# Depthwise convolution: six of its 47 half-length taps as ScalarE products, summed by adding DMAs; contiguous even and odd accumulators

## The chip, the cores and the metric

The program runs on one core of a Trainium2 chip. Five engines work side by side, each through its own queue in order: TensorE (PE, matrix products), VectorE (DVE), ScalarE (ACT), GpSimd (POOL) and SyncE (SP). SP and POOL issue the DMA transfers. An instruction that waits for a semaphore holds back everything behind it in its own queue. The metric is the device time of one execution in microseconds (us).

## What is computed

One step of a hybrid decoder layer, for a prompt of 1024 positions and 8 sample requests of 8 positions each. The part that the change touches is branch B, a causal depthwise convolution with 31 taps over 1024 channels, between a gated product and a LayerNorm:

```python
xn = rmsnorm(x, norm1_g)
q, k, v, glu_a, glu_b, gate_a, gate_b = split(xn @ w_in)
branch_a = swa_attention(q, k, v, sinks) @ w_o_attn
u = glu_a * sigmoid(glu_b)
c = dwconv_valid(concat([conv_b_past, u]), conv_b_w, conv_b_bias)   # 31 taps per channel
branch_b = silu(layernorm(c, ln_b_g, ln_b_b)) @ w_pb
h = x + (sigmoid(gate_a) * branch_a + sigmoid(gate_b) * branch_b) @ w_out
y = h + conv_ffn(rmsnorm(h))
```

All arithmetic is float32. Each product of matrices is made of three (high by high, high by low, low by high), and this is why TensorE has so much to do.

## The kernel before

**Stages.** The first 640 us are the input projection with everything that hangs on it: weights are taken one 128-column block after another, each multiplied with all 1088 positions (in chunks of 384, 384 and 320) into PSUM banks, of which there are four under the tag `mm` and four under `aux`. What leaves the banks is rounded and split into two words by ACT and DVE (`q`, `k`, `v`) or turned into the gated input `u`. The LayerNorm and the other projections follow, and the second half of the run is the convolutional FFN.

**The convolution.** Channels are taken in 8 tiles of 128, on the partitions. When `u` of tile i is complete, `a_done` calls `conv(i, u)` with a low priority (`CONV_LATER`), so that the scheduler strews its instructions among those of the projections and, from some 200 us on, of attention. The eight convolutions follow each other from 66 to 619 us. Even and odd positions are computed apart by three sums of half length, 512 positions: `bt` (even inputs by even taps, 513 wide), `ye` (odd inputs by odd taps), `yo` (sums of neighbouring inputs, `sm`, by sums of neighbouring taps, `hsum`). That is 16 + 15 + 16 = 47 taps of half length instead of 62. The first tap of each sum is written by ACT (L555 to L557); the other 44 are multiply-adds on DVE (`mac`, L545), each reading and writing its accumulator. `ye` and `yo` are the even and odd columns of one tile `c`, so their elements are two apart; `bt` is a tile of its own. Then the sums are combined into `out`, inside `u` (L565 to L567), and POOL stores it to DRAM as `d_c` (L568, L569). The LayerNorm (`ln_steps`, L571 on) loads `d_c` once the last of the eight stores has landed.

**What stands around it in the queues.** On DVE: the low words of weights (`wlo`, L183) and of `q` and `k` (L787, L809), the softmax (L392, an instruction of its own kind), the low words of the transposed probabilities (`ptl`, L237). On ACT: the high words (L182, L786, L236), the exponentials (L397), their scaling (L401). On POOL: a copy of a column for each softmax (`p<-nsink`, L386), the stores of the gates (L767), of attention (L468, L469), loads of cached keys and values (L479, L480) and the stores of the convolution. Tiles of a tag are reused in turn: `u` has two buffers, `p` two, `c`, `sm` and `bt` one each.

Adding DMAs exist in the kernel at three other places, all later: L1202 (`ml` from DRAM into SBUF), L1463 through L1456 (`d_b`, from SBUF to DRAM) and L1919 (`H`).

Of the kernel before, what the change touches and what calls it, by code (L numbers as in the profile page):

```python
# [8 lines left out]
AF = mybir.ActivationFunctionType  # L9
ALU = mybir.AluOpType  # L10
AX = mybir.AxisListType

P = 128
DM = 1024
KT = DM // P
SEQ = 1024
# [64 lines left out]
SQUARES_LATER = 3000  # L81
W_PARTS = 4
CONV_LATER = 1200
TURN_SOONER = -60
LN_AT = ((0, 1, 17, 36), (2, 37, 50, 80), (60, 81, 103, 134), (90, 135, 152, 183))
LEAD = (0, 0)
# [42 lines left out]
class Build:  # L129
# [273 lines left out]
    def attn_unit(self, p, blk, st):  # L403
# [22 lines left out]
        def turn(g, kb):  # L426
# [5 lines left out]
            pl = self.t(self.at, [P, 512], "ptl", F32R, bufs=2)  # L432
            with self.later(TURN_SOONER if self.now - self.gated <= 3 else 0):
                self.split_ps(ph, pl, ps)
# [98 lines left out]
    def conv(self, i, u):  # L533
        nc = self.nc
        half = SEQ // 2
        acc = self.t(self.cv, [P, T], "c")
        sm = self.t(self.cv, [P, half + 15], "sm")
        bt = self.t(self.cv, [P, half + 1], "bt")
        us = u[:, PW:].rearrange("p (b t) -> p b t", b=NB)
        sp = acc[:, SEQ:].rearrange("p (b t) -> p b t", b=NB)  # L540
        ev, od = u[:, 0:PW:2], u[:, 1:PW:2]
        ye, yo = acc[:, 0:SEQ:2], acc[:, 1:SEQ:2]
        h = lambda k: self.c("cw", i * CW + k)
        hs = lambda j: self.hsum[:, 16 * i + j:16 * i + j + 1]
        mac = lambda o, x, w: nc.vector.scalar_tensor_tensor(o, x, w, o, ALU.mult, ALU.add)  # L545
        taps = self.c("cw", i * CW, CW)[:, None, None, :].to_broadcast([P, NB // 2, NT, CW])
        prod = acc[:, 0:NS // 2 * CW].rearrange("p (b t k) -> p b t k", b=NB // 2, k=CW)
        for x in range(2):
            win = us[:, 4 * x:4 * x + 4, 0:NT]
            win = bass.AP(tensor=win.tensor, offset=win.offset, ap=[list(z) for z in win.ap] + [[1, CW]])  # L550
            nc.vector.tensor_tensor(prod, win, taps, ALU.mult)
            nc.vector.tensor_reduce(sp[:, 4 * x:4 * x + 4, :], prod, AX.X, ALU.add)
        nc.vector.tensor_tensor(sm, od[:, 0:half + 15], ev[:, 1:half + 16], ALU.add)
        act = nc.scalar.activation
        act(bt, ev[:, 0:half + 1], AF.Identity, scale=h(0))  # L555
        act(ye, od[:, 0:half], AF.Identity, bias=self.c("cb", i), scale=h(1))
        act(yo, sm[:, 0:half], AF.Identity, bias=self.cb2[:, i:i + 1], scale=hs(0))  # L557
        for j in range(1, 16):
            mac(bt, ev[:, j:j + half + 1], h(2 * j))
            if j < 15:  # L560
                mac(ye, od[:, j:j + half], h(2 * j + 1))
            mac(yo, sm[:, j:j + half], hs(j))
        out = u[:, NS:NS + SEQ]
        nc.vector.tensor_scalar(u[:, 0:NS], acc[:, SEQ:], self.c("cb", i), None, ALU.add)
        nc.vector.tensor_tensor(yo, yo, bt[:, 1:], ALU.subtract)  # L565
        nc.vector.tensor_tensor(out[:, 1::2], yo, ye, ALU.subtract)
        nc.vector.tensor_tensor(out[:, 0::2], ye, bt[:, 0:half], ALU.add)  # L567
        nc.gpsimd.dma_start(self.d_c[i, :, 0:SEQ], out)  # L568
        nc.gpsimd.dma_start(self.d_c[i, :, SEQ:], u[:, 0:NS])  # L569
# [123 lines left out]
    def phase_x(self):  # L693
# [46 lines left out]
        def a_done(i, u):  # L740
            us = u_views(u)
            nc.gpsimd.dma_start(a["o_cbp"][i], u[:, SEQ:SEQ + HIST])
            nc.gpsimd.dma_start(a["o_cbs"][i], us[:, :, NT:])
            with self.later(CONV_LATER):
                self.conv(i, u)
# [1443 lines left out]
```

## Time and profile before

| | us |
|---|---|
| median of 3 runs | 1640.43 (1640.31 to 1640.95) |
| span of the profiled execution | 1640.2 |
| PE busy | 1631.0 |
| DVE busy | 1401.0 |
| ACT busy | 880.5 |
| POOL busy | 262.9 |
| the 352 MACs of the convolutions (L545), busy | 262.8 |

The profiled execution's own time was that of its span, 1640.2 us from the first instruction to the last, and the granted TensorE clock was 0.999 over it. A row of a group names the line, the engine, the operation, the tile written and those read, shapes and count; then its busy time and the mean of one in ns; then the idle time in front and what ended most of it. A row of the timeline has the start in us and the duration, and in square brackets the idle time before it, if there was any. `L545` is line 545 of the kernel before. In the new kernel the lines up to `conv` stand 2 further down, the conv's `mac` is L547, its starts L557 to L559, and from its combining sums on all lines stand 12 further down (L809 is L821).

### The profile page before, as it was taken

To read this page: it belongs to the slowest core of one execution; us is meant where nothing else is said; L and a number is where in the kernel's file an instruction comes from. 1 tells how busy PE (TensorE), PEld (TensorE's weight loads), DVE (VectorE), ACT (ScalarE), POOL (GpSimd) and SP (SyncE) were. 2 spreads that over 40 slices of the span, in tenths; PEclk is the share of its full clock that TensorE was granted. 3 is DMA by queue.
4 is the path that set the end of the run, shared out by engine and by line. 5 is a ranking of instruction groups with operands and counts; after the bars stand their busy time and mean duration, and the time that the engine had idled before them with its cause. 6 is when DMAs were issued, how large, how long until landed. Compare 5 with 4: busy or idle time off the path is not lost.

```text
span 1640.2 us, 30212 instructions
## 1 busy us (share of the span) xinstructions
PE 1631.0 (99%) x11540; PEld 1615.4 (98%) x11540; DVE 1401.0 (85%) x2597; ACT 880.5 (54%) x1845; POOL 262.9 (16%) x549
## 2 busy tenths in 40 slices
PE   9999999999999999999999999999999999999998
PEld 9999999999999999999999999999999999999998
DVE  7899979999979996778755999988888887989867
ACT  6524277774488754666532465555555555524322
POOL 0100111222011101111102422222222111000000
PEclk9999999999999999999999999999999999999999
DMA  6221222323121256548763631344444334766423
GB/s 211 85 59 54 64 74 58 106 83 114 43 70 42 90 181 196 174 152 233 185 226 108 214 119 63 112 117 115 115 117 118 99 112 142 255 165 163 110 62 110
DMA packets 104857, 201.58 MB, mean 123 GB/s; under 512 B 25992, under 2 KB 56712, under 8 KB 104696
## 3 DMA queue, kind: packets, MB, share of 16 engines
q1 hardware_dynamic: 81528, 131.47, 26.4%
q0 software_dynamic: 22752, 67.79, 13.8%
q8 instruction: 90, 1.47, 0.4%
q14 instruction: 55, 0.45, 0.1%
q10 hardware_dynamic: 432, 0.40, 0.1%
HBM read 137.55 MB, written 64.03 MB: 123 GB/s over the span
## 4 chain that ended last, share of the span: by engine, by line
PE 89%; DVE 5%; ACT 3%; DMA 1%; issue 1%; SPq 0%; POOLq 0%; DVEq 0%; ACTq 0%
PE mm L201 21%; PE mm L202 21%; PE mm L203 21%; PE aux L203 7%; PE aux L202 7%; PE aux L201 7%; PE aux L430 1%; DVE c L545 1%; PE aux L443 1%; PE aux L444 1%; DMA ct<-d_c 1%; PE aux L420 1%; PE aux L421 1%; DVE bt L545 1%; ACT ct L625 1%
## 5 line engine op out<-in xcount | busy, mean ns | idle before, releaser
L201 PE MATMUL mm<-xh,whi 128*128 128x384 f32 (+1 forms) x904 | 301.4, 333 | 0.3 <-ACT xh L290 0.3
L202 PE MATMUL mm<-xl,whi 128*128 128x384 f32 (+1 forms) x904 | 295.3, 327 | 0.2 <-DVE xl L291 0.2
L203 PE MATMUL mm<-xh,wlo 128*128 128x384 f32 (+1 forms) x904 | 295.4, 327 | 0.0
L202 PEld LDWEIGHTS mm<-xl,whi 128*128 128x128 f32 x904 | 170.0, 188 | 1.2 <-DVE xl L291 0.5
L201 PEld LDWEIGHTS mm<-xh,whi 128*128 128x128 f32 x904 | 169.9, 188 | 1.3 <-ACT xh L290 0.6
L203 PEld LDWEIGHTS mm<-xh,wlo 128*128 128x128 f32 x904 | 169.7, 188 | 0.1
L1435 DVE SCALAR_TENSOR_TENSOR acc<-st,fc,acc 128x1104 f32<-128x1104 f32 x88 | 119.9, 1365 | 12.2 <-issue 6.7
L182 ACT CAST whi<-wraw 128x1024 fp32r<-128x1024 f32 (+1 forms) x62 | 59.6, 967 | 65.2 <-PE mm L202 51.3
L203 PE MATMUL mm<-th,wlo 128*128 128x272 f32 x320 | 92.4, 289 | 0.0
L201 PE MATMUL mm<-th,wlo 128*128 128x272 f32 x320 | 92.4, 289 | 0.0
L202 PE MATMUL mm<-tl,wlo 128*128 128x272 f32 x320 | 92.4, 289 | 0.0
L545 DVE SCALAR_TENSOR_TENSOR bt<-u,consts,bt 128x513 f32<-128x513 f32 x120 | 89.7, 748 | 0.7
L545 DVE SCALAR_TENSOR_TENSOR c<-sm,hsum,c 128x512 f32<-128x512 f32 x120 | 89.5, 746 | 0.7
L203 PE MATMUL mm<-mh,wlo 128*128 128x272 f32 (+4 forms) x304 | 89.2, 293 | 0.0
L545 DVE SCALAR_TENSOR_TENSOR c<-u,consts,c 128x512 f32<-128x512 f32 x112 | 83.6, 746 | 0.5
L236 ACT CAST whi<-wraw 128x512 fp32r<-128x512 f32 x76 | 47.5, 625 | 61.5 <-DVE wraw L1631 26.4
L183 DVE TENSOR_TENSOR wlo<-wraw,whi 128x1024 fp32r<-128x1024 f32 (+1 forms) x62 | 68.9, 1116 | 7.2 <-ACT whi L182 6.9
L1780 ACT COPY st<-mm 128x272 f32<-128x272 f32 (+2 forms) x132 | 43.8, 349 | 56.9 <-PE mm L203 56.9
L236 ACT CAST wlo<-wraw 128x512 fp32r<-128x512 f32 x76 | 47.4, 624 | 40.7 <-PE mm L203 17.9
L397 ACT ACTIVATE p<-p,nm 128x257 f32<-128x257 f32 (+1 forms) x128 | 62.3, 490 | 11.9 <-DVE nm L392 11.4
L1433 ACT ACTIVATE acc<-st,fc 128x1104 f32<-128x1104 f32 x44 | 57.6, 1314 | 15.3 <-DVE st L1736 11.9
L201 PE MATMUL aux<-mh,whi 128*128 128x272 f32 (+4 forms) x216 | 63.9, 296 | 0.0
(712 smaller groups left out, 5764.9 us busy)
## 6 DMA issues: line engine op xcount, KB each, us to landing
wraw<-wall SPq DMA_DIRECT2D x118, 512.0 KB, 3.8
bw<-d_b SPq DMA_DIRECT2D x42, 272.0 KB, 3.8
d_b<-gd POOLq DMA_DIRECT2D x36, 272.0 KB, 6.1
d_b<-acc POOLq DMA_DIRECT2D x24, 272.0 KB, 4.9
ar<-wdn SPq DMA_DIRECT2D x32, 192.0 KB, 3.8
d_g<-acc POOLq DMA_DIRECT2D x10, 544.0 KB, 4.4
ga<-d_ga SPq DMA_DIRECT2D x8, 544.0 KB, 5.2
ct<-d_c SPq DMA_DIRECT2D x8, 544.0 KB, 6.3
```

The costliest lines, as they stand in the source:

```text
L182: self.cast = self.nc.scalar.copy(h[:, z], r[:, z]).ins
L183: self.nc.vector.tensor_tensor(l[:, z], r[:, z], h[:, z].bitcast(F32), ALU.subtract)
L201: mm(ps, wh, xh, start=first, stop=False, skip_group_check=more)
L202: mm(ps, wh, xl, start=False, stop=False, skip_group_check=more)
L203: self.last_mm = mm(ps, wl, xh, start=False, stop=last, skip_group_check=more).ins
L236: self.cast = self.nc.scalar.copy(h, src).ins
L397: nc.scalar.activation(pt[:, j, lo:width + 1], pt[:, j, lo:width + 1], AF.Exp, bias=nm[:, j:j + 1], scale=-1.0, accum_out=den[:, j:j + 1])
L420: nc.tensor.matmul(ps[:, j, :], q[g][:, h, qs], kd[g][:, keys], start=True, stop=False)
L545: mac = lambda o, x, w: nc.vector.scalar_tensor_tensor(o, x, w, o, ALU.mult, ALU.add)
L1433: nc.scalar.activation(acc, st[:, 0:AW], AF.Identity, bias=fb(f), scale=fw(f, 0))
L1435: nc.vector.scalar_tensor_tensor(acc, st[:, k:k + AW], fw(f, k), acc, ALU.mult, ALU.add)
L1780: self.evicted = (add if second and n == 0 and j == 1 else op)(d, r(banks[bank, j]))
```

## The change

Two constants and some fifteen lines in `conv`:

```diff
+ADDED = 6
+TAPS_FIRST = 8
...
-        ye, yo = acc[:, 0:SEQ:2], acc[:, 1:SEQ:2]
+        ye, yo = acc[:, 0:half], acc[:, half:SEQ]
...
         act(yo, sm[:, 0:half], AF.Identity, bias=self.cb2[:, i:i + 1], scale=hs(0))
+        added = ADDED if i else 0
+        for j in range(1, added + 1):
+            tap = self.t(self.at, [P, half], "tap", bufs=2)
+            act(tap, sm[:, j:j + half], AF.Identity, scale=hs(j))
+            nc.gpsimd.dma_start(yo, tap, accum_op=ALU.add)
+        left = list(range(added + 1, 16))
         for j in range(1, 16):
             mac(bt, ev[:, j:j + half + 1], h(2 * j))
             if j < 15:
                 mac(ye, od[:, j:j + half], h(2 * j + 1))
-            mac(yo, sm[:, j:j + half], hs(j))
+            if j > (TAPS_FIRST if added else 0):
+                x = left.pop(0)
+                mac(yo, sm[:, x:x + half], hs(x))
+        for x in left:
+            mac(yo, sm[:, x:x + half], hs(x))
```

In convolutions 1 to 7 (not in 0), taps 1 to 6 of the odd sum `yo` are no longer MACs. ACT multiplies `sm` by the tap into a buffer `tap`, and a DMA from POOL's queue adds the buffer to `yo`, in SBUF. There are two buffers. The other nine MACs of `yo` come later among those of `bt` and `ye`: none before the ninth pair. `ye` and `yo` are the two halves of `c`, each contiguous; `out` is still written in alternating columns. ADDED and TAPS_FIRST are the number of taps so treated and the number of pairs ahead of the first odd MAC.

**VectorE, convolution 1, where its first odd MAC now stands.** `c<-u` is a MAC of the even sum, `c<-sm` one of the odd sum, `bt` the third; `kl` and `q` are low words from the projection. Before:

```order
L545 SCALAR_TENSOR_TENSOR bt_1265<-u_1085,consts_77,bt_1265 128x513
L787 TENSOR_TENSOR q_28_123<-mm_1483,q_28_123 64x256
L545 SCALAR_TENSOR_TENSOR c_1263<-u_1085,consts_77,c_1263 128x512
L545 SCALAR_TENSOR_TENSOR c_1263<-sm_1264,hsum_86,c_1263 128x512
L809 TENSOR_TENSOR kl_143_1517<-mm_1525,kd_141_1515 64x384
```

Now:

```order
L185 TENSOR_TENSOR wlo_153_1534<-wraw_1431,whi_152_1533 128x1024
L799 TENSOR_TENSOR q_27_122<-mm_1495,q_27_122 64x256
L547 SCALAR_TENSOR_TENSOR bt_1265<-u_1085,consts_77,bt_1265 128x513
L799 TENSOR_TENSOR q_28_123<-mm_1495,q_28_123 64x256
L547 SCALAR_TENSOR_TENSOR c_1263<-sm_1264,hsum_86,c_1263 128x512
L547 SCALAR_TENSOR_TENSOR c_1263<-u_1085,consts_77,c_1263 128x512
L821 TENSOR_TENSOR kl_149_1529<-mm_1537,kd_147_1527 64x384
```

Before, an odd MAC stands here that is one of many; now this `c<-sm` is the first of the convolution and waits for the sixth adding DMA, ahead of the same low word of `k`.

**ScalarE, convolution 1, behind the odd sum's start** (`c<-sm` with the bias `cb`). Before:

```order
L557 ACTIVATE c_1263<-sm_1264,cb_17_85,hsum_86 128x512
L786 CAST q_28_123<-mm_1359 64x384
L182 CAST whi_135_1421<-wraw_1324 128x1024
L786 CAST q_27_122<-mm_1388 64x256
L786 CAST q_28_123<-mm_1388 64x256
```

Now:

```order
L559 ACTIVATE c_1263<-sm_1264,cb_17_85,hsum_86 128x512
L798 CAST q_28_123<-mm_1371 64x384
L184 CAST whi_141_1433<-wraw_1336 128x1024
L798 CAST q_27_122<-mm_1400 64x256
L563 ACTIVATE tap_1280<-sm_1264,hsum_86 128x512
L798 CAST q_28_123<-mm_1400 64x256
L804 COPY qs_124<-mm_1400 64x4x2x8 x2
L563 ACTIVATE tap_1283<-sm_1264,hsum_86 128x512
```

The products `tap` stand among the casts that empty the PSUM banks; the two rows shown are the third and fourth product, whose buffers the first and second adding DMA must have read.

**GpSimd, convolution 3**, where it runs beside attention; the semaphores in brackets are those that a row waits for (DMASW: a DMA of this queue). Before:

```order
L767 DMA d_ga_60<-gt_2837 128x384 [waits DMASW5_49,Activation_49]
L767 DMA d_ga_60<-gt_2928 128x320 [waits Activation_49]
L386 COPY p_3122<-nsink_84 128x4 [waits PE_49,Pool_49]
L386 COPY p_3174<-nsink_84 128x4 [waits PE_49,Activation_49,Pool_49]
L479 DMA kp_3551<-kpT 128x256 [waits DMASW0_49,PE_49]
```

Now:

```order
L779 DMA d_ga_60<-gt_2873 128x384 [waits Activation_49]
L564 DMA c_2697<-tap_2708 128x512 [waits DMASW2_49,DVE_49,Activation_49]
L564 DMA c_2697<-tap_2711 128x512 [waits DMASW2_49]
L564 DMA c_2697<-tap_2714 128x512 [waits DMASW4_49,DMASW3_49,Activation_49]
L779 DMA d_ga_60<-gt_2964 128x320 [waits DMASW5_49,Activation_49]
L388 COPY p_3158<-nsink_84 128x4 [waits PE_49,Pool_49]
L564 DMA c_2697<-tap_2717 128x512 [waits DMASW6_49,DMASW4_49,Activation_49]
L388 COPY p_3210<-nsink_84 128x4 [waits PE_49,Pool_49]
L481 DMA kp_3599<-kpT 128x256 [waits DMASW7_49,PE_49]
L564 DMA c_2697<-tap_2720 128x512 [waits DMASW6_49,DMASW0_49,Activation_49]
```

The adding DMAs, each with a wait for a DMA of the same queue, now stand between the store of a gate, the softmax columns and the load of cached keys.

## The prediction

> **What bounds the kernel now.** I read the page's totals first, then the chain of work that ended last, then a table of the stages.
>
> ```profile
> span 1640.2 us, 30212 instructions
> PE 1631.0 (99%) x11540; PEld 1615.4 (98%) x11540; DVE 1401.0 (85%) x2597; ACT 880.5 (54%) x1845; POOL 262.9 (16%) x549
> PE 89%; DVE 5%; ACT 3%; DMA 1%; issue 1%; SPq 0%; POOLq 0%; DVEq 0%; ACTq 0%
> ```
>
> TensorE (PE) is busy 1631.0 of 1640.2 us. A change can take away at most the other 9.2 us, plus waits too short to show; it can add whatever it makes TensorE wait. So the question is not how many VectorE (DVE) instructions go, but whether TensorE ever waited for them in the stage where they stand. The stage is 65 to 620 us. The columns are the stretch, its length, then busy time and (count) for PE, PEld, DVE, ACT, POOL, the granted clock, the DMA share and GB/s:
>
> ```profile
> 120.00:180.00 60.00, 60.00 (x372) 60.00 (x371) 55.76 (x82) 25.53 (x52) 4.91 (x12) 1.00 0.24 69
> 300.00:360.00 60.00, 60.00 (x391) 58.15 (x391) 58.47 (x132) 46.09 (x118) 13.90 (x24) 1.00 0.23 72
> 420.00:480.00 60.00, 59.71 (x372) 57.83 (x371) 48.25 (x105) 39.17 (x98) 3.81 (x11) 1.00 0.16 50
> 480.00:540.00 60.00, 59.94 (x394) 58.12 (x393) 58.09 (x137) 48.27 (x127) 8.59 (x17) 1.00 0.24 56
> ```
>
> VectorE is 80 to 97% full here, yet TensorE is idle 0.29 + 0.06 us. The ledger of TensorE's waits over the whole run agrees: the only one near this stage comes after it, when the LayerNorm that follows the convolutions reads their stored result.
>
> ```profile
> PE aux L591 <- DVE sm L583: 1.2, 1, 1.2
> ```
>
> **What the change takes away.**
>
> ```profile
> L545 DVE SCALAR_TENSOR_TENSOR c<-sm,hsum,c 128x512 f32<-128x512 f32 x120 | 89.5, 746 | 0.7
> 139.19 0.75 DVE L545 SCALAR_TENSOR_TENSOR c<-sm,hsum,c 128x512 f32<-128x512 f32 x1
> 139.85 0.75 DVE L545 SCALAR_TENSOR_TENSOR bt<-u,consts,bt 128x513 f32<-128x513 f32 x1
> 140.52 0.75 DVE L545 SCALAR_TENSOR_TENSOR c<-u,consts,c 128x512 f32<-128x512 f32 x1
> ```
>
> Six multiply-adds (MACs) leave each of convolutions 1 to 7, 42 in all. One lasts 0.746 us, but starts follow each other after 0.66 to 0.67, so VectorE gets back 42 x 0.665 = 28 us. At the end that is worth next to nothing: the windows show 0.35 us of TensorE idle in the stage, and the LayerNorm's 1.2 us are to be had only if the last convolution is stored sooner. Records that are busy can hide small pacing losses, so I take a gain of 2 us; the bounds are 0 and 4. Making the even and odd accumulators contiguous I cost at nothing, between -0.05 and +0.05 us a MAC: `c<-u,consts,c`, which steps by two, takes the same 0.75 us as `bt`, which is contiguous. If contiguity did speed up a MAC, it would be hidden like the 28 us.
>
> **What it adds on ScalarE (ACT).** 42 products with a scale, 128x512. The nearest row is the odd accumulator's start, the same instruction with a bias:
>
> ```profile
> L557 ACT ACTIVATE c<-sm,cb,hsum x8: 845/858/875, 75.6 to 572.8; 128x512 f32<-128x512 f32 x8
> ```
>
> 42 x 0.86 = 36 us, 5.2 us per convolution. ACT is 43% full at 120 to 180 and 77 to 80% at 300 to 360 and 480 to 540, so the work fits; what matters is where it stands in the queue (below).
>
> **What it adds as DMA.** 42 adding DMAs of 256 KB from GpSimd's (POOL's) queue, SBUF to SBUF. All six of one convolution have the same destination, and each waits until the one before has landed: a chain of six. This trace has no adding DMA inside SBUF, so I bound one from both sides.
>
> ```profile
> d_ga<-gt POOLq DMA_DIRECT2D x16, 192.0 KB, 2.1
> d_c<-u POOLq DMA_DIRECT2D x8, 512.0 KB, 3.2
> bw<-d_b SPq DMA_DIRECT2D x42, 272.0 KB, 3.8
> ml<-d_ma POOLq DMA_DIRECT2D x12, 272.0 KB, 5.0
> ...
> L1202 POOL DMA_DIRECT2D ml<-d_ma x12: 850/859/911, 751.2 to 802.9; - x12
> DMA to landing us min/median/max: 4.1/5.0/6.7
> ```
>
> - Below: a plain store of POOL's takes 2.1 us for 192 KB and 3.2 for 512, so 2.3 for 256. An adding issue occupies POOL 0.86 us (L1202) where plain ones take 0.54 (below), so 2.6 us if adding itself is free.
> - Above: `ml<-d_ma` is an adding DMA of 272 KB, DRAM to SBUF, with a median of 5.0.
> - Between: the plain load of 272 KB from DRAM takes 3.8, so adding costs 1.2. A second look gives the same size. L1456 stores five 272 KB pieces in a row; the DMA issues of 1125 to 1129 us, where all are plain, then of 1061 to 1068, where the three of `gd` add:
>
> ```profile
> d_b<-gd POOLq DMA_DIRECT2D x3, 272.0 KB, 5.3
> ...
> d_b<-gd POOLq DMA_DIRECT2D x3, 272.0 KB, 8.2
> ```
>
> The middle one of the three has itself and one other adding DMA in front: (8.2 - 5.3) / 2 = 1.4. So 2.3 + 1.2 to 1.4 = 3.5 to 3.7 alone on the queues; with weight loads beside it I take D = 3.9 us, and 0.1 for POOL to see the landing: a period of 4.0, a chain of 24.0 us.
>
> The Trainium skill ("DMA: Bandwidth & Descriptors", section "Anatomy of one DMA — SWDGE (gpsimd) path") fits 2.0 us plus the bytes over 436 GB/s to a GpSimd DMA, an estimate of 2.6 us here. The trace disagrees for adding: the 272 KB ones would be 2.6 by it, and none of twelve landed below 4.1. By the fit the sum would be that of the first rival.
>
> **Where the chain meets the path.** The first odd MAC, now behind the sixth landing, stands after 17 or more other MACs. What covers the chain is VectorE's work from the first even MAC to it. In convolution 1:
>
> ```profile
> 128.79 0.75 DVE L545 SCALAR_TENSOR_TENSOR c<-u,consts,c 128x512 f32<-128x512 f32 x1
> ...
> 148.86 0.75 DVE L545 SCALAR_TENSOR_TENSOR c<-sm,hsum,c 128x512 f32<-128x512 f32 x1
> 149.64 0.55 DVE L809 TENSOR_TENSOR kl<-mm,kd 64x384 fp32r<-64x384 f32 x1
> ...
> L183 DVE TENSOR_TENSOR wlo<-wraw,whi 128x1024 fp32r<-128x1024 f32 x2 | 2.4, 1217 | 0.0
> L787 DVE TENSOR_TENSOR q<-mm,q 64x384 fp32r<-64x384 f32 x6 | 3.3, 556 | 0.2
> L787 DVE TENSOR_TENSOR q<-mm,q 64x256 fp32r<-64x256 f32 x4 | 1.7, 422 | 0.1
> ```
>
> 17 x 0.665 + 2 x 1.22 + 5 x 0.556 + 4 x 0.422 = 18.2 us. The chain starts 0.85 later (after the odd accumulator's start), so the wait is 0.85 + 24.0 - 18.2 = 6.6 us. Behind it on VectorE stand `kl<-mm`, which frees PSUM banks, and `wlo`, the next weights. TensorE's reserve there: the cast of `kd` ended at 158.82, and the matmul that takes its bank began at 162.40, the narrowest of this stage. The rows below give these 3.6 us; for convolution 2 (a bank of `v`, L237) 197.62 - 190.17 = 7.4, for convolution 5 (L815) 419.02 - 414.65 = 4.4, and beside attention 0.5 after the second `ptl` (L237 to L444).
>
> ```profile
> 158.34 0.48 ACT L810 CAST kd<-mm 64x384 fp32r<-64x384 f32 x1
> 162.40 0.31 PE L201 MATMUL mm<-xh,whi 128*128 128x320 f32 x1
> ...
> 189.75 0.42 DVE L237 TENSOR_TENSOR v<-mm,v 128x256 fp32r<-128x256 f32 x1
> 197.62 0.28 PE L201 MATMUL mm<-whi,xh 128*128 128x256 f32 x1
> ...
> 414.38 0.27 ACT L815 COPY gt<-mm 128x128 f32<-128x128 f32 x1
> 419.02 0.34 PE L201 MATMUL mm<-xh,whi 128*128 128x384 f32 x1
> ...
> 316.58 1.29 DVE L237 TENSOR_TENSOR ptl<-aux,pth 128x512 fp32r<-128x512 f32 x2
> 318.35 0.40 PE L444 MATMUL aux<-ptl,v 128*128 128x512 f32 x1
> ```
>
> The loss in convolution 1 is 6.6 - 3.6 = 3.0. The other six I sum the same way, with the instructions in the new order at the same durations. Cover: 17.8, 24.7, 29.7, 17.8, 31.2 and 23.1 us; the chain starts 1.1, 2.3, 7.6, 0.8, 3.9 and 2.4 after the first even MAC. Waits: 7.3, 1.6, 1.9, 7.0, none, 3.3. Less the reserves: convolution 2 loses nothing, 5 loses 2.6, and 3, 4 and 7, beside attention, for which I take a reserve of 1 us (an estimate, above the row's 0.5 since VectorE has 4 us less of its own to do there), 0.6, 0.9 and 2.3. Together 3.0 + 0.6 + 0.9 + 2.6 + 2.3 = 9.4.
>
> **The two queues that the chain blocks.** There are two buffers of products, so the third product waits for the first add's landing, and casts and exponentials queue behind it. In convolution 1 ACT comes some 4 us late, inside the wait already counted. POOL waits through each landing, and copies a column that softmax needs:
>
> ```profile
> L386 POOL COPY p<-nsink x32: 184/192/2289, 203.4 to 575.8; 128x4 f32<-128x4 f32 x32
> L767 POOL DMA_DIRECT2D d_ga<-gt x24: 540/540/581, 42.5 to 626.9; - x24
> ...
> 273.99 0.82 POOL L386 COPY p<-nsink 128x4 f32<-128x4 f32 x1 [0.79 <-PE aux L430]
> 278.45 0.19 POOL L386 COPY p<-nsink 128x4 f32<-128x4 f32 x1 [3.64 <-PE aux L430]
> ```
>
> Nine such copies stand between adds of convolutions 3, 4, 6 and 7. Each may come up to one landing, 4 us, late, but most find the add before them landed: in convolution 3 the two fall 4.5 us apart. With 5.2 us more on ACT at 80%, I take a third of a us for each, 3 in all (bounds 0 and 10).
>
> **Sum.** 1640.2 + 9.4 + 3 - 2 = 1650.6, say 1651. The span, 1640.2, stands 0.2 below the median of the runs, 1640.43.
>
> **Rivals.**
>
> 1. *The adds are short and all is hidden* (D up to 3.3). At 2.6 the period is 2.7 and the chain 16.2: 0.85 + 16.2 is under 18.2, nobody waits. At 3.3 the chain is 20.4, and convolution 1's wait of 3.0 stays inside its 3.6. For it: the plain stores' 2.1. Against: 4.1 as the least of twelve adding ones. Time: 1640.4 less 0 to 4, about 1638.5. Only its better half counts as faster.
> 2. *The other end*: D = 5.0, the median of `ml<-d_ma`. The chain is 30.6; waits 13.2, 13.9, 8.2, 8.5, 13.6, 3.3, 9.9; less the reserves 51 us in all: 1689, and some of it caught up between convolutions, 1680. For it: that row. Against: its source is DRAM.
> 3. *The queues in attention cost more than the wait of the odd MACs*: with D below 3.3 but 10 us from POOL's copies and ACT's queue, 1640.4 + 10 - 2 = 1648. For it: copies of 0.19 us stretched to 2.29. Against: the 4.5 us between copies above. The Trainium skill ("SBUF — State Buffer", section on the ports) has DVE and GpSimd shut each other out of a shared port, which such stretched copies would agree with; no run here shows the cause.
>
> **How the numbers follow.** Forecast 0.37, rival 1 0.32, rival 2 0.14, rival 3 0.17. The range reaches from rival 1's middle, 1637, to rival 2's, 1680. About 0.2% (3.3 us) is what can be told from no change: faster means below 1637.1, slower above 1643.7. Rival 1 gives a third of its chance to faster (0.10) and the rest to same (0.22); the small ends of the forecast and of rival 3 give 0.07 more to same; slower has 0.61.
>
> **What would show it.** Each add's time from issue to landing: 3.9 right, under 3.3 rival 1, 5 rival 2. VectorE idle in front of the first odd MAC, ended by the DMA: 6 to 7 us in convolutions 1, 2 and 5, 0 to 3 in the others. TensorE's waits: 1 to 3 us by L809 or L183 near 165 and 410, and by L237 or L401 near 350 and 600. VectorE's busy time down by 28 to 31, ScalarE's up by 36. The forecast is wrong if the adds land early, or if banks give TensorE more reserve than the narrowest pair of rows says.

## The result, and the profile after

The changed kernel takes 1668.4 us (median of 4 runs, 1666.0 to 1671.5) against 1640.7 beside it: a ratio of 1.0166, 95% interval 1.0154 to 1.0178, or 27.7 us slower. Slower was forecast, and the range held the time, but 10.6 us had been forecast. In the profiled execution the span is 1668.5.

```profile
span 1668.5 us, 30296 instructions
PE 1641.2 (98%) x11540; PEld 1621.7 (97%) x11540; DVE 1374.9 (82%) x2555; ACT 906.5 (54%) x1887; POOL 300.0 (18%) x591
PE 70%; ACT 3%; DMA 2%; DVE 2%; issue 1%; POOL 0%; POOLq 0%; ACTq 0%; DVEq 0%
```

VectorE has 26 us less to do and ScalarE 26 more, as meant. But the same 11540 matmuls keep TensorE busy for 10 us longer, and it is idle 18 us longer. Where it waits, from the ledger of TensorE's waits, and the adding DMAs' own line with who waited for them:

```profile
PE aux L446 <- DVE ptl L239: 7.4, 3, 4.7
PE mm L203 <- ACT gt L827: 5.3, 1, 5.3
PE mm L203 <- ACT kd L822: 2.8, 2, 1.7
PE aux L445 <- ACT pth L238: 2.6, 2, 1.8
...
  POOL c L564: 45.9, 16
  ACT tap L563: 31.3, 17
  DVE c L547: 14.4, 6
...
DMA to landing us min/median/max: 3.2/3.3/6.1
```

To see where the time goes, I set each matmul's start beside the start of the same matmul before. TensorE's lag grows at the convolutions and nowhere else:

| convolution | lag gained, us | forecast | adds: issue of the first to landing of the sixth | VectorE's wait at the first odd MAC | forecast |
|---|---|---|---|---|---|
| 1 | 4.2 | 3.0 | 26.2 | 1.5 | 6.6 |
| 2 | 9.2 | 0 | 25.0 | 4.5 | 7.3 |
| 3 | 0.7 | 0.6 | 24.5 | 0.7 | 1.6 |
| 4 | 3.6 | 0.9 | 23.7 | 0.1 | 1.9 |
| 5 | 7.9 | 2.6 | 27.7 | 4.5 | 7.0 |
| 6 | 0 | 0 | 28.4 | 1.1 | 0 |
| 7 | 3.1 | 2.3 | 24.6 | 2.2 | 3.3 |

The sum is 28.7; later 0.8 comes back. Convolution 2 alone makes a third of it. VectorE there (with one row of ACT), then TensorE, from the timeline of the changed kernel:

```profile
192.06 0.74 DVE L547 SCALAR_TENSOR_TENSOR c<-u,consts,c 128x512 f32<-128x512 f32 x1
...
207.42 0.72 ACT L563 ACTIVATE tap<-sm,hsum 128x512 f32<-128x512 f32 x1 [2.77 <-DMA c<-tap]
208.44 0.42 DVE L239 TENSOR_TENSOR v<-mm,v 128x256 fp32r<-128x256 f32 x1 [1.34 <-ACT v L238]
...
212.99 0.08 DVE L394 DVE_READ_ACCUMULATOR2_ANT nm<- 128x1 f32 x1
217.51 0.75 DVE L547 SCALAR_TENSOR_TENSOR c<-sm,hsum,c 128x512 f32<-128x512 f32 x1 [4.45 <-DMA c<-tap]
...
226.03 0.25 DVE L576 TENSOR_SCALAR u<-c,consts 128x64 f32<-128x64 f32 x1
...
229.63 1.22 DVE L185 TENSOR_TENSOR wlo<-wraw,whi 128x1024 fp32r<-128x1024 f32 x1
230.76 0.68 DVE L239 TENSOR_TENSOR ptl<-aux,pth 128x512 fp32r<-128x512 f32 x1
...
231.50 0.79 PE L446 MATMUL aux<-ptl,v 128*128 128x512 f32 x1 [4.69 <-DVE ptl L239]
233.27 0.52 PE L204 MATMUL mm<-xl,whi 128*128 128x384 f32 x1
```

and VectorE in the kernel before:

```profile
187.77 0.74 DVE L545 SCALAR_TENSOR_TENSOR c<-u,consts,c 128x512 f32<-128x512 f32 x1
...
218.29 1.22 DVE L183 TENSOR_TENSOR wlo<-wraw,whi 128x1024 fp32r<-128x1024 f32 x1
219.43 0.69 DVE L237 TENSOR_TENSOR ptl<-aux,pth 128x512 fp32r<-128x512 f32 x1
...
225.13 0.24 DVE L564 TENSOR_SCALAR u<-c,consts 128x64 f32<-128x64 f32 x1
```

VectorE waits for the sixth landing at 217.51. Between there and `ptl`, the low word that attention's product needs, stand the nine odd MACs, the rest of the others and even the first combining sums: 13.2 us without a gap. Before, `ptl` stood ahead of those sums; but that order is not what makes it late. From the first even MAC of `c` (187.77 before, 192.06 now) up to `ptl`, VectorE has 63 instructions in both kernels, 31.6 us of work before and 31.3 now. What is new is idle time in that stretch, 7.4 us against 0.04: 4.45 in front of the first odd MAC, and 2.9 in front of low words of `v`, whose casts stand on ACT behind products that wait for a landing. So the landing sets the time of `ptl`, and of TensorE. Then the matmuls that follow take 0.52 us where the same ones took 0.33 before. Stretches around five stalls, with the granted clock third from the end:

```profile
160.00:163.00 3.00, 1.96 (x11) 1.96 (x12) 2.94 (x5) 1.46 (x3) 0.00 (x0) 1.00 0.00 0
231.00:233.00 2.00, 1.50 (x6) 1.32 (x7) 1.10 (x3) 0.58 (x1) 0.49 (x1) 0.50 0.50 143
233.00:235.00 2.00, 2.00 (x8) 2.00 (x8) 1.32 (x2) 0.59 (x1) 0.25 (x2) 0.50 0.86 352
237.00:239.00 2.00, 2.00 (x12) 1.91 (x12) 0.96 (x5) 2.00 (x9) 0.00 (x0) 1.00 0.44 61
373.00:377.00 4.00, 2.46 (x11) 1.69 (x10) 4.00 (x6) 2.63 (x5) 1.89 (x4) 0.91 0.69 141
442.00:444.00 2.00, 1.53 (x5) 1.53 (x6) 1.88 (x4) 1.35 (x5) 1.13 (x2) 0.50 0.04 16
446.00:448.00 2.00, 2.00 (x8) 2.00 (x7) 1.94 (x4) 0.64 (x2) 0.00 (x0) 0.51 0.00 0
620.00:623.00 3.00, 3.00 (x13) 2.92 (x12) 2.96 (x6) 0.83 (x2) 0.57 (x1) 0.66 0.09 34
```

Four times, at convolutions 2, 4, 5 and 7, the granted clock is at half for 3.4 to 5.5 us of the matmuls behind a stall. Against the usual spacing of the same matmuls, the halved stretches cost 2.35 + 1.84 + 2.60 + 1.75 = 8.5 us. Between 60 and 680 us TensorE is idle for 19.1 us, against 0.4 before. 19 + 8.5 is the 28.

### The profile page after: what moved, and what is told of

Read it like the earlier page. It is cut to its first block, busy times and chain, and to the rows that moved or that the text cites. A ratio compares the mean times of both kernels' runs of the same rounds, so it can differ in the third digit from the quotient of the medians.

```text
span 1668.5 us, 30296 instructions
## 1 busy us (share of the span) xinstructions
PE 1641.2 (98%) x11540; PEld 1621.7 (97%) x11540; DVE 1374.9 (82%) x2555; ACT 906.5 (54%) x1887; POOL 300.0 (18%) x591
## 4 chain that ended last, share of the span: by engine, by line
PE 70%; ACT 3%; DMA 2%; DVE 2%; issue 1%; POOL 0%; POOLq 0%; ACTq 0%; DVEq 0%
PE mm L205 16%; PE mm L203 16%; PE mm L204 16%; PE aux L205 6%; PE aux L204 6%; PE aux L203 6%; DMA c<-tap 2%; ACT p L399 1%; ACT p L403 1%; PE aux L432 0%; DVE c L547 0%; PE aux L446 0%; PE aux L445 0%; DVE wlo L185 0%; PE aux L422 0%
## 5 line engine op out<-in xcount | busy, mean ns | idle before, releaser
L547 DVE SCALAR_TENSOR_TENSOR c<-sm,hsum,c 128x512 f32<-128x512 f32 x78 | 58.0, 744 | 15.0 <-DMA c<-tap 14.4
L1445 ACT ACTIVATE acc<-st,fc 128x1104 f32<-128x1104 f32 x44 | 57.6, 1314 | 14.4 <-DVE st L1748 11.9
```

The lines of the kernel that those rows point to most:

```text
L1445: nc.scalar.activation(acc, st[:, 0:AW], AF.Identity, bias=fb(f), scale=fw(f, 0))
```

## The experiments

Each was timed beside the kernel before; the ratio is to that one, with its 95% interval. The theory at the start was that the chain of six landings holds VectorE at the first odd MAC. The rivals were that the queues of ACT and POOL, held by the same chain, cost more; or that each add costs its share of traffic or work.

**Contiguous accumulators alone.**

```diff
-ADDED = 6
+ADDED = 0
```

> No tap is treated specially (ADDED = 0); only the even and odd accumulators are contiguous. Theory 1 (the loss comes from the chain of six landings): 1640.7 as before, within 2 us, and a MAC of 0.745 us as before. Rival (the layout itself costs, through the interleaving of the output or a longer MAC): some of the 28 us is here already.

1641.0 us, ratio 0.9997 (0.9987 to 1.0007): no change. The MACs of the even sum, now contiguous, take 746 ns as before.

```profile
L547 DVE SCALAR_TENSOR_TENSOR c<-u,consts,c 128x512 f32<-128x512 f32 x112 | 83.5, 746 | 0.5
```

**Three, four and five taps.** `ADDED = 3`, `4` and `5`.

> Three taps instead of six in each of convolutions 1 to 7 (ADDED = 3): one chain of three landings, 11.5 us. Theory 1 (a threshold: the chain is shorter than the cover): 1639 to 1642, not half of the loss. Rival 3 (each add or product costs its share, in ACT's queue or as DMA traffic): half of the loss, about 1654.

> Four taps instead of six in convolutions 1 to 7. The chain is four landings, 4 x 3.83 = 15.3 us from the trace of the changed kernel, or 17.9 with one slow landing, against the smallest cover of 17.8. Theory B (threshold): before + 0 to 3 us. Linear rival (each add costs its share of 28 us): before + 18.

> Five taps. The chain is 19.2 us, or 21.7 with one slow landing: VectorE waits 2 to 5 us in convolutions 1, 2 and 5 and hardly in the others. Theory B, with the reserve beside attention near nothing and half clock after the stalls: before + 8 to 14. Linear rival: before + 23.

| taps | 0 | 3 | 4 | 5 | 6 |
|---|---|---|---|---|---|
| us | 1641.0 | 1641.9 | 1648.1 | 1659.5 | 1668.4 |
| ratio | 0.9997 | 1.0004 | 1.0039 | 1.0112 | 1.0166 |

The ratios' intervals are within 0.0015 either way. Three adds per convolution, half of the work, cost nothing; each one above costs 6 to 11 us. That is a threshold and not a share. It lies lower than expected: four were to cost at most 3 us and cost 6.7, five cost 18 where 8 to 14 were expected. The wait of VectorE for the landings (us, times, longest) in the profile with four taps, then in that with five:

```profile
DVE c L547 <- DMA c<-tap: 2.5, 1, 2.5
...
DVE c L547 <- DMA c<-tap: 14.1, 6, 4.4
```

With four, the one wait is in convolution 2, because the first odd MAC there came after 16 MACs and four other instructions only, not 21 and 14: presumably the scheduler expects a shorter chain and puts the odd MACs sooner. VectorE's wait is not all of these 6.7 us: in convolution 4 TensorE stands 1.7 us although VectorE waits for no landing there, and ACT waits 16.6 us for landings in all. So the cover that I had counted in the changed kernel's order holds for that order alone.

**The adds go to a scratch tile.** VectorE waits for none.

```diff
...
-            nc.gpsimd.dma_start(yo, tap, accum_op=ALU.add)
+            nc.gpsimd.dma_start(dump, tap, accum_op=ALU.add)
```

> The six adds go to a scratch tile that nobody reads, so the six odd taps of convolutions 1 to 7 are left out of the output; ACT writes that tile's start (7 instructions of 0.86 us more). The chain of six landings, ACT's waits for a buffer and POOL's waits are all still there; VectorE waits for none of them. Theory 1 (VectorE held at the first odd MAC is the main cost): the waits of 14.4 us on VectorE go, and the time falls to 1640 to 1648. Rival 2 (the blocked queues of ACT and POOL cost most): stays at 1658 or more.

1664.7 us, ratio 1.0141 (1.0126 to 1.0156). Most of the loss stays, 23 of 28 us, so VectorE's wait is not needed for it. Convolution 2 on ACT in this kernel:

```profile
190.24 0.72 ACT L566 ACTIVATE tap<-sm,hsum 128x512 f32<-128x512 f32 x1 [6.45 <-DMA dump<-tap]
194.07 0.72 ACT L566 ACTIVATE tap<-sm,hsum 128x512 f32<-128x512 f32 x1 [2.85 <-DMA dump<-tap]
194.95 0.86 ACT L558 ACTIVATE c<-u,consts 128x512 f32<-128x512 f32 x1
```

A product waits for a buffer that the first landing must free, and the start of the even sum (L558) stands behind it: 194.95, where it was 186.10 before and 190.39 in the changed kernel, in which TensorE was 4.2 us behind by then. All even MACs are late, and with them everything behind them, `ptl` too. In the changed kernel L558 stands ahead of the waiting products. So this run shows that ACT's wait can cost as much, not that it did in the changed kernel.

**Which wait?** Three kernels separate them. Four buffers of products instead of two (meant to free ACT of nearly all its waits; about half of them stayed); adding slices of `sm` instead of products (ACT entirely free, VectorE still waits); the same into the scratch tile (neither waits). A fourth computes the products alone.

```diff
-            tap = self.t(self.at, [P, half], "tap", bufs=2)
+            tap = self.t(self.at, [P, half], "tap", bufs=4)
```

> Four buffers of products instead of two; all else as in the changed kernel. The fifth product waits for the first landing, the sixth for the second, so ACT's waits (31 us in the changed kernel) should all but vanish; the chain of six and VectorE's wait behind it stay. Theory A (ACT's queue, held by the products, is the main cost; the scratch run, in which VectorE did not wait, lost 23 us all the same): 1640 to 1648. Theory B (each of the two waits, ACT's and VectorE's, costs nearly all of it alone, since both end with the chain): 1655 to 1668.

```diff
-            nc.gpsimd.dma_start(yo, tap, accum_op=ALU.add)
+            nc.gpsimd.dma_start(yo, sm[:, j:j + half], accum_op=ALU.add)
```

> The DMAs add the unscaled slices of sm itself, not ACT's products, so six odd taps are wrong in the output; ACT still computes its 42 products but no product waits for a landing. POOL's waits and VectorE's wait at the first odd MAC stay. It is the counterpart of the scratch run. Theory A: 1640 to 1648. Theory B: 1655 to 1668. It should agree with the run with four buffers.

```diff
...
-            nc.gpsimd.dma_start(yo, tap, accum_op=ALU.add)
+            nc.gpsimd.dma_start(dump, sm[:, j:j + half], accum_op=ALU.add)
```

> Both cuts: the DMAs add slices of sm into the scratch tile; six odd taps are left out of the output. Neither ACT nor VectorE waits for a landing; the 42 DMAs, POOL's waits for them and ACT's 42 products (and 7 starts) stay. Theories A and B: 1640 to 1644. Rival C (POOL's queue, its softmax copies behind the adds, or the DMA traffic): 1650 or more.

```diff
-            nc.gpsimd.dma_start(yo, tap, accum_op=ALU.add)
```

> The 42 products on ACT alone, with no DMA; six odd taps are left out of the output. All theories: 1639 to 1642, since nothing waits for anything new; if it is slower, ACT's 36 us themselves cost. If it is faster than before by over 3 us, VectorE's 28 us had been worth something.

| kernel | ACT waits for landings | VectorE waits | us | ratio (95%) |
|---|---|---|---|---|
| as changed | 31.3 | 14.4 | 1668.4 | 1.0166 (1.0154 to 1.0178) |
| four buffers | 16.6 | 29.0 | 1675.1 | 1.0215 (1.0195 to 1.0234) |
| from `sm` | 0 | 42.9 | 1683.6 | 1.0260 (1.0244 to 1.0275) |
| into scratch | 42.5 | 0 | 1664.7 | 1.0141 (1.0126 to 1.0156) |
| from `sm` into scratch | 0 | 0 | 1648.4 | 1.0045 (1.0030 to 1.0060) |
| products only | 0 | 0 | 1642.2 | 1.0007 (0.9997 to 1.0016) |

The waits are those of the profiled execution; with four buffers that was the slowest of the four runs, 1681.2. VectorE's wait in the kernel that adds from `sm`:

```profile
DVE c L547 <- DMA c<-sm: 42.9, 6, 9.9
```

Theory A, that ACT's queue was the main cost, falls: freeing ACT made it slower. VectorE alone, held by the chain, is enough (from `sm`); ACT alone is enough for most of it (into scratch); with neither, 7 us are left. That is theory B, but the two kernels with less of ACT's wait lost more than the changed one. Part of that is order again: in convolution 6 VectorE had 69 instructions between its first even and first odd MAC as changed, and 37 in both of these. There the lag gained was nothing as changed, and 6.8 and 5.9 us in these two:

```profile
PE aux L504 <- ACT av L499: 7.0, 2, 5.0
```

That row is of the kernel with four buffers; 5.0 us of it are at 555.8, in convolution 6. That the scheduler places the odd MACs by when it expects the adds is read from the orders, not tested by itself.

The 42 products on ACT cost nothing that can be measured, and the 28 us taken from VectorE bring nothing either. What is left with neither wait shows at POOL's queue, in convolution 6 of the kernel that adds from `sm` into scratch:

```profile
500.54 0.86 POOL L567 DMA_DIRECT2D dump<-sm  x1 [2.98 <-DMA dump<-sm]
501.08 0.89 POOL L782 DMA_DIRECT2D d_ga<-gt  x1
501.64 0.53 POOL L388 COPY p<-nsink 128x4 f32<-128x4 f32 x1
502.20 0.51 ACT L399 ACTIVATE p<-p,nm 128x257 f32<-128x257 f32 x1 [3.49 <-POOL p L388]
504.68 0.50 PE L445 MATMUL aux<-pth,v 128*128 128x512 f32 x1 [2.02 <-DVE av L452]
```

An add waits 2.98 us for the one before it; behind it the softmax column is late, and an exponential waits 3.49 us for it; ACT's casts for attention's product stand behind that, and TensorE waits 2.02 us. In all, ACT waits 6.8 us for two such columns in this kernel and for none with the products alone. The kernel with the products alone moves none of the adds' bytes either, so these two runs do not tell the traffic from POOL's queue; but three adds per convolution, half of those bytes, cost nothing.

**Two chains instead of one.** Taps 1, 3, 5 into the odd accumulator, 4 and 6 into the product of tap 2, and one more VectorE addition.

```diff
...
-            nc.gpsimd.dma_start(yo, tap, accum_op=ALU.add)
+            nc.gpsimd.dma_start(yo if j % 2 else z, tap, accum_op=ALU.add)
...
+            nc.vector.tensor_tensor(yo, yo, z, ALU.add)
```

> The same six taps on ACT, all in the output, but summed in two chains: taps 1, 3, 5 are added to the odd accumulator, taps 4 and 6 to the product of tap 2, and VectorE adds the two (0.68 us more per convolution). Five adds instead of six, the longest chain three landings, 3 x 3.83 = 11.5 us from the trace of the changed kernel, under the smallest cover of 17.8. Theory 1: no wait at the first odd MAC, 1640 to 1644. Rival 2 (queues): five adds still hold POOL, but each for half as long; 1650 or more.

> Two chains (five adds) as in the earlier run, with three buffers of products instead of two, so that the products wait for earlier landings; in the earlier run ACT waited 19 us for landings and TensorE lost 8. Theory B (what was left there was ACT's queue): before + 0 to 3. Rival C (POOL's queue, whose cost showed as 7 us where neither ACT nor VectorE waited): before + 5 to 9.

1649.9 us with two buffers, ratio 1.0052 (1.0037 to 1.0067): a third of the loss, with the same six taps. But not the 1640 to 1644 hoped for: with two chains on one queue, adds were in flight beside each other and took up to 7.2 us, and the chain was 14 to 22 us long, not 11.5. VectorE waited 2.4 us in all for landings and ACT 20.9; which of them costs the 8.5 us that are left, no run shows. With three buffers it is 1655.4, ratio 1.0083 (1.0068 to 1.0098), against both expectations. ACT in convolution 2 of that kernel:

```profile
189.33 0.72 ACT L567 ACTIVATE tap<-sm,hsum 128x512 f32<-128x512 f32 x1 [4.30 <-DMA z<-tap]
189.96 0.35 ACT L238 CAST v<-mm 128x256 fp32r<-128x256 f32 x1
190.22 0.85 ACT L558 ACTIVATE c<-u,consts 128x512 f32<-128x512 f32 x1
```

The additional buffer let the scheduler put products ahead of the accumulators' starts, and then the one that waits holds L558, at 190.22, where two buffers had it at 187.62. It is the order of the scratch run again; that it explains the difference is read from this row, not tested.

**Only convolutions 1, 2 and 5.**

```diff
-        added = ADDED if i else 0
+        added = ADDED if i in (1, 2, 5) else 0
```

> Six taps, but in convolutions 1, 2 and 5 alone; 3, 4, 6 and 7 as with contiguous accumulators. In the trace of the changed kernel TensorE fell behind by 4.2, 9.2 and 8.0 us at these three, 21 of 28. Theory B (the loss belongs to the convolutions whose cover is shortest): before + 17 to 22. Rival (attention's convolutions, through POOL's and ACT's queues): before + 8 or less.

1659.1 us, ratio 1.0106 (1.0089 to 1.0123): 17.7 us over the kernel before, at the lower end of the expectation. These three, where the cover is shortest, carry most of it; those beside attention, whose cover is longer, the rest. By convolution the lag grows by 4.4, 9.7 and 3.7 us here: 1 and 2 lose what they lost in the changed kernel, 5 less than half of its 7.9.

## Why the prediction was wrong

- **That it is PE-bound and the 28 us of VectorE are worth nothing:** right. I had taken a gain of 2 us; products alone and three taps gave none.
- **ACT's 36 us:** 42 products took 0.72 us each, 30 us, not 0.86: the row with a bias was the nearest but not the same. They lie beside other work, as said: 1642.2.
- **Contiguity at nothing:** right, 1641.0.
- **The adding DMA at 3.9 us, period 4.0, chain 24.0:** near in sum (the chains' mean is 25.7), wrong in its parts, and that the errors offset each other is luck. A lone add landed in 3.3 us (median; least 3.2). From a landing to the next issue POOL mostly took 0.52, not the 0.1 that no row stood behind, so the period is 3.8. Ten of the 42 took over 4 us, the longest 6.1. A weight load of 512 KB was in flight beside five such slow ones (5.8 to 6.1 us), itself landing in 4.2 to 4.6; in convolution 2 two stores were in flight as well. The chains were 23.7 to 28.4.
- **VectorE's waits:** forecast 27.7 us in all, 14.4 measured. They are shorter because ACT, held by its own products, made VectorE wait before it came to the odd MAC; the chain's end is what counts, and not who waits for it. With ACT's part, VectorE's idle time up to the first odd MAC (gaps over 0.3 us) was 7.6, 7.3 and 9.8 us in convolutions 1, 2 and 5, where 6.6, 7.3 and 7.0 were forecast: the delay was right in 2, near in 1 and too short in 5.
- **"Less the reserves: convolution 2 loses nothing":** the step that failed. I set the wait of 7.3 against the reserve of the nearest PSUM bank, 7.4 us for `v`. But VectorE is an in-order queue with no gap from the first odd MAC to `ptl`, 13.2 us later. A delay on it is not used up by a bank that is free early: it travels along the queue to the first place where TensorE is close behind, and that was `ptl`, with some half a us. I had quoted that row, and used it for convolutions 3, 4 and 7 only. By it convolution 2 would have lost some 6.8 of the 7.3; its two stalls were 1.8 and 4.7 us.
- **Convolution 5, 2.6 forecast:** here the reserve held, and the chain was too short in the sum. Two of its adds took 5.8 and 6.0 us, and it took 27.7 us, not 24.0. The cast that frees the bank ended at 414.65 before; it stood behind casts that waited for `kl`, which VectorE reached only after the odd MAC. Now it ends at 442.42, 27.8 us later than before. TensorE's lag was 17.9 by then, so the cast is 9.8 us late; less the 4.4 of reserve that is 5.4, and TensorE stood 5.3:

```profile
440.00 0.75 DVE L547 SCALAR_TENSOR_TENSOR c<-sm,hsum,c 128x512 f32<-128x512 f32 x1 [4.52 <-DMA c<-tap]
440.78 0.43 DVE L821 TENSOR_TENSOR kl<-mm,kd 64x256 fp32r<-64x256 f32 x1
441.24 0.37 ACT L822 CAST kd<-mm 64x256 fp32r<-64x256 f32 x1 [4.73 <-DVE kl L821]
442.15 0.27 ACT L827 COPY gt<-mm 128x128 f32<-128x128 f32 x1
442.47 0.69 PE L203 MATMUL mm<-xh,whi 128*128 128x384 f32 x1 [5.33 <-ACT gt L827]
```

- **What was not in the sum:** the halved clock after the stalls, 8.5 us. Before, no stall was longer than 1.2 us, and no window of the stage showed less than 1.00.
- **The two queues at 3:** ACT's waits, which I took as lying inside VectorE's, can be most of the loss by themselves; POOL's showed as up to 7 us without them, inside the bounds of 0 to 10.

So of the 17.1 us missed, 8.5 are the clock, and the rest is TensorE's idle time, 19.1 us where 9.4 + 3 - 2 = 10.4 were forecast. Convolution 2 has 6.5 of it where nothing was forecast, convolution 5 has 5.3 where 2.6 was, and the other five together 7.3 where 6.8 were. Rival 2 (D = 5.0, 1680 and more) would have come nearer from the other side, but the adds were shorter than forecast, not longer.

## What to carry to other kernels

A wait in an in-order queue is paid at the tightest consumer behind it (13 us behind it here), until the queue has had that much idle time; look for the least reserve among all that stand behind, not for that of the next one. A chain of transfers that wait for each other costs its landings plus the issuing engine's reaction each time (3.3 + 0.5 us here), and it holds every queue that feeds it: measure the threshold (here three adds per convolution) before using more. On this kernel, which is bound by TensorE, freeing VectorE was worth nothing, and a stall can cost more than its length (8.5 us on top of 19 here).

## What was not expected of the hardware

- **The clock after a stall.** Around stalls of 4.7 and 5.3 us the granted clock was halved, for 4.8 and 5.5 us of the matmuls behind them, at a cost of 2.35 and 2.60; so it was, for 3.4 us each, at a stall of 2.0 near 617 and at two of 0.8 and 0.7 us near 375, where TensorE was busy 2.46 of 4 us. Two of 1.7 and 1.1 us in convolution 1, 5 us apart, left it at 1.00 (row 160 to 163). The Trainium skill ("TensorE: Matmul & The Clock Gate", section "Part 1: The HAM clock gate") says the same of the two rates, and that the gate looks at windows of about 3.4 us. The trace agrees with the half rate (0.50) and, with 3.4 to 5.5 us, the time to recover; but an idle time under 3.4 us was enough here, so a window need not be wholly idle.
- **The adding DMA inside SBUF.** 256 KB in 3.3 us from issue to landing (median; 3.2 the least); the issue itself keeps POOL for 0.85. The estimate of 2.6 us by the Trainium skill's fit ("DMA: Bandwidth & Descriptors", section "Anatomy of one DMA — SWDGE (gpsimd) path") is too short by 0.7 for it, and the chain's period is longer by another 0.5.
